# S5 output matrices built on VectorE behind the scan, and query decays broadcast through DRAM

## The chip, the cores and the metric

The kernel is one launch on one core of a Trainium2 chip. A core has five engines that each run their own stream of instructions in order: TensorE (PE in the profile, with its weight loads as PEld), VectorE (DVE), ScalarE (ACT), GpSimd (POOL) and SyncE (SP), which here only issues DMA transfers; POOL and ACT issue some too. Engines wait for one another through semaphores. The metric is the device time of one execution in microseconds, as a median over runs.

## What is computed

One step of a hybrid layer for 128 prompt tokens and 1024 sample tokens, model width 1024, in float32. Cut to what matters here:

```python
h    = norm(x) * (1 + sc1) + sh1
proj = h @ w_in                                   # 1024 x 2560
q, k, v, g, u = split(proj)                       # 4 x retention of 512, S5 input of 512
o_ret = bidirectional_retention(q, k, v, log_sigmoid(ret_decay), state_ret)
#   scores * exp(lg * (i - j));  states read with exp(lg * (i + 1)), written with exp(lg * (chunk - 1 - j))
y, s5_re, s5_im = bidirectional_s5(u, a, log_dt, b, c, d, s0)
#   s[t] = exp(a dt) s[t-1] + b u[t] (64 complex states, 32 groups of 16 channels); y = Re(c s) + d u
y = gelu(y); y = y * sigmoid(y @ w_glu + b_glu)
x = ln1(alpha * x + g1 * (concat(o_ret * silu(g), y) @ w_out))
x = ln2(alpha * x + g2 * squared_relu_mlp(norm(x) * (1 + sc2) + sh2))
```

## The kernel before

Each engine runs its instructions in the order in which the program writes them. For the stretch that matters (about 130 to 455 us of the span) that order comes from `weave` at the program's line 1097: it takes several tracks, each a generator that yields how many microseconds the piece just written should last, and always goes on with the track whose clock is lowest. The yields are numbers written by hand; they set the order and nothing else.

The tracks are these.

- `units(4, 20)`: the input projection, one unit for every 128 columns of `w_in`. A unit is three groups (384 tokens each) of 24 matmuls, `pu` at L205 to L207: eight blocks of the model width, three passes each, since weights and activations are split into a high and a low part. The split of the weights of unit i+1 is one copy `wh` on ACT (L197) and one subtraction `wl` on DVE (L198); the load `wr` of unit i+2 is issued on SP (L311). The first four units, which carry the S5 input u, are done before.
- `chain(s5_scan(), spill(), s5_w2_rest(), tables())`: the S5 scan on DVE. Seven steps over rows of SB, four operations of 128x1152 each (L667 to L670), 16 short steps on 128x64 (L684 to L687), and seven more of four row operations (L705 to L708). `spill` writes the scanned states to DRAM (SD, L890) and the final states to the output. `tables` makes the retention decays: the eight columns kd, and, as rows over 128 positions, RT (eight query decays) and DM (four decay matrices), in four batches of 128x384 through `emit_exp`, a chain of 16 DVE operations (L121 to L131).
- `mod_round(2, ...)`: eight pairs of matmuls `pm` (L266) with the modulation weights wa.
- `chain(s5_w2(), y_track(4))`: `build(u, d)` makes the output matrix W of channel block u and direction d (128x1152; twelve operations of 128x288, L978 to L980) on POOL for the first six of the eight and, through `s5_w2_rest`, on DVE after the scan for the last two. `finish(u, d)` multiplies it with Y on PE (`pK`, L992 and L993), writes W to DRAM (WD, L995) and after both directions the kernel matrix Kp (KD, L1011). Then `y_track`: `y_load(u)` issues on SP the loads of block u, eight of KD (L1056), the S5 input X from XD (L599), two of WD (L1062) and two of SD (L1063), into the buffers `late` and `ub`; `s5_y(u)` runs on PE 24 matmuls `py` (L1075 to L1077, eight groups of three, the third of each with the second W and states), on ACT the gelu, and POOL's queue writes YD and reads it back transposed (yT).

There is one set of these buffers. So the loads of block u+1 wait on SP until the matmuls of block u are done with them, and X of block u+1, which lies in the buffer that takes block u's gelu, until YD(u) has been written. After the weave PE goes on with the retention scores `psc` (L1129).

Of the kernel before, what the change touches and what calls it, by code (L numbers as in the profile page):

```python
# [9 lines left out]
F32 = mybir.dt.float32  # L10
# [7 lines left out]
P = 128  # L18
# [6 lines left out]
G = 32  # L25
# [6 lines left out]
def kernel(  # L32
# [52 lines left out]
    def t384(name, dt=F32):  # L85
        return sm.tile([P, 384], dt, tag="h", name=nm(name), bufs=4)

    def t512(name):
        return sm.tile([P, 512], F32, tag="rows", name=nm(name), bufs=1)

    def ct(name, shape, dt=F32):
        return const.tile(list(shape), dt, name=nm(name))

    def bc(ap, axis, n):
        ap = ap.unsqueeze(axis)
        shp = list(ap.shape)
        shp[axis] = n
        return ap.to_broadcast(shp)
# [11 lines left out]
    def chain(*tracks):  # L110
        for t in tracks:
            yield from t
# [542 lines left out]
    def s5_scan():  # L655
# [10 lines left out]
        for m in range(2, 9):  # L666
            tt(t1, bc(LRf, 3, NSB), row(m - 1), MUL)  # L667
            tt(row(m), row(m), t1, ADD)
            tt(t1, bc(LIf, 3, NSB), swp(row(m - 1)), MUL)
            tt(row(m), row(m), t1, ADD)  # L670
            yield 5.6

        R5 = SB.rearrange("p r d l (k s) -> p r d l k s", s=NSB)
        zr = st_[:, 0:64].rearrange("p (r d l) -> p r d l", r=2, d=2)
# [28 lines left out]
        for m in range(1, 8):  # L703
            prev = row(0) if m == 1 else cr
            tt(t1, bc(LIf, 3, NSB), swp(prev), MUL)  # L705
            tt(cr, bc(LRf, 3, NSB), prev, MUL)
            tt(cr, cr, t1, ADD)
            tt(row(m), row(m), cr, ADD)  # L708
            yield 5.6
        rel(st_, SE_)  # L710


# [190 lines left out]
        yield 0.0  # L903


    kd, kx = ct("kd", [P, 16]), ct("kx", [P, 48])
    RTf, DMf = ct("RT", [P, 1024]), ct("DM", [P, 512])
    RT = RTf.rearrange("p (a i) -> p a i", a=8)
    DM = DMf.rearrange("p (h i) -> p h i", h=4)
# [1 line left out]
    def tables():  # L911
# [15 lines left out]
        stt(lgb, p_, -2.0, m_, MUL, ADD)  # L927
        yield 3.0

        ts(kx[:, 0:4], lgb[:, 0:4], posP[:, 1:2], None, MUL)  # L930
        ts(kx[:, 4:8], lgb[:, 4:8], posP[:, 0:1], None, MUL)
        ts(kx[:, 8:16], lgb, 128.0, None, MUL)
        emit_exp(kd, kx[:, 0:16], kx[:, 16:32], kx[:, 32:48])
        yield 3.0

        pr = t512("pr")
        px, rx = pr[:, 0:256], pr[:, 256:512]
        ts(px[:, 0:128], posI, 1.0, None, ADD)
        ts(px[:, 128:256], posI, -1.0, 128.0, MUL, ADD)
        ts(rx[:, 0:128], posI, posP[:, 0:1], None, SUB)  # L940
        ts(rx[:, 128:256], rx[:, 0:128], -1.0, 0.0, MUL, ALU.max)
        ts(rx[:, 0:128], rx[:, 0:128], 0.0, None, ALU.max)
        x, t, k = (t384("tx") for _ in range(3))
        rows = [(RTf, a) for a in range(8)] + [(DMf, h) for h in range(4)]
        for i in range(4):
            part = rows[3 * i:3 * i + 3]
            for j, (f, a) in enumerate(part):
                xv = x[:, j * P:(j + 1) * P]
                if f is RTf:
                    ts(xv, px[:, 0:128] if a < 4 else px[:, 128:256], lgb[:, a:a + 1], None, MUL)  # L950
                else:
                    ts(xv, rx[:, 0:128], lgb[:, a:a + 1], None, MUL)
                    stt(xv, rx[:, 128:256], lgb[:, 4 + a:5 + a], xv, MUL, ADD)
            emit_exp(x, x, t, k)
            for j, (f, a) in enumerate(part):
                V.tensor_copy(f[:, a * P:(a + 1) * P], x[:, j * P:(j + 1) * P])
            yield 6.0
        tt(DM, DM, bc(ident, 1, 4), ADD)


# [2 lines left out]

    Ws, pks = {}, {}

    def build(u, d, e=PO.tensor_tensor):
        T = Ws[u, d] = slot("W2")
        Tv = T.rearrange("p (g k c) -> p g k c", g=8, k=9)
        for g in range(0, 8, 2):
            gs = slice(d * G + u * 8 + g, d * G + u * 8 + g + 2)  # L970
            gx = slice(u * 8 + g, u * 8 + g + 2)
            a_r, a_i = Ar[:, :, gs], Ai[:, :, gs]
            if d == 1:
                a_r, a_i = a_r[:, ::-1], a_i[:, ::-1]
            a_r, a_i = (bc(z.rearrange("p k g -> p g k"), 3, 16) for z in (a_r, a_i))
            Zv = t384("Z2")[:, 0:288].rearrange("p (g k c) -> p g k c", g=2, k=9)
            Tg = Tv[:, g:g + 2]
            e(Tg, a_r, bc(X1[:, gx], 2, 9), MUL)  # L978
            e(Zv, a_i, bc(X2[:, gx], 2, 9), MUL)
            e(Tg, Tg, Zv, ADD)  # L980

    def finish(u, d):
        extra[0] += 0.65
# [27 lines left out]
            ld(KD[u].rearrange("(s q) c x -> q c s x", q=4)[q], Kp[32 * q:32 * q + 16])  # L1011

    seq2 = [(u, d) for u in range(4) for d in range(2)]
    NPW, done = 6, []

    def s5_w2():

        for i, k in enumerate(seq2[0:NPW]):
            build(*k)
            yield 13.5  # L1020
            if i:
                finish(*seq2[i - 1])
        finish(*seq2[NPW - 1])
        while len(done) < 8 - NPW:
            yield 1.0
        for k in seq2[NPW:]:
            finish(*k)
        yield 3.0

    def s5_w2_rest():  # L1030
        for k in seq2[NPW:]:
            build(*k, tt)
            yield 6.5
            done.append(k)


    YD = drp.tile([4, 8, P, NCOL], F32, name="YD")
# [56 lines left out]
            yield YL2  # L1094

    YL1, YL2, NY = 22.0, 2.0, 4
    weave(units(4, 20), chain(s5_scan(), spill(), s5_w2_rest(), tables()), mod_round(2, 12.0, 60.0), chain(s5_w2(), y_track(NY)))
    rel(*hTh, *hTl)
    if stop <= 3:
        return  # L1100
# [611 lines left out]
```

## Time and profile before

| | us |
|---|---|
| runs (median of three) | 1500.23 (1498.35 to 1500.4) |
| the profiled execution: its own time | 1500.58 |
| the profiled execution: span | 1498.8 |
| PE busy over the span | 1385.7 (92%) |
| DVE busy | 839.1 (56%) |
| POOL busy | 317.2 (21%) |
| mean granted clock of PE | 0.963 |

PE is busy for nine tenths of the whole span, but that is an average over stages. The change lies in the stage from 130 to about 480 us, so the rows below are read from there. In the timeline of PE a row's duration overlaps with the next row's; the distance between starts is what a matmul costs. A count x2 or x8 in a row stands for that many hardware instructions merged into one.

### The profile page before, as it was taken

To read this page: it belongs to the slowest core of one execution; us is meant where nothing else is said; L and a number is where in the kernel's file an instruction comes from. 1 tells how busy PE (TensorE), PEld (TensorE's weight loads), DVE (VectorE), ACT (ScalarE), POOL (GpSimd) and SP (SyncE) were. 2 spreads that over 40 slices of the span, in tenths; PEclk is the share of its full clock that TensorE was granted. 3 is DMA by queue.
4 is the path that set the end of the run, shared out by engine and by line. 5 is a ranking of instruction groups with operands and counts; after the bars stand their busy time and mean duration, and the time that the engine had idled before them with its cause. 6 is when DMAs were issued, how large, how long until landed. Compare 5 with 4: busy or idle time off the path is not lost.

```text
span 1498.8 us, 19700 instructions
## 1 busy us (share of the span) xinstructions
PE 1385.7 (92%) x7630; PEld 1239.3 (83%) x7630; DVE 839.1 (56%) x1468; ACT 585.2 (39%) x973; POOL 317.2 (21%) x297
## 2 busy tenths in 40 slices
PE   5778997698988989999999999999999999999996
PEld 2468886598988778887999999989999998899995
DVE  6774699959304677677344443664443356543345
ACT  3434411012213563225344544444445444444451
POOL 0734586600214531253000010010001001000002
PEclk9789898799999999999999999999999999999998
DMA  9413344276786415138534434347443334734321
GB/s 327 99 58 97 116 151 134 80 181 197 185 198 241 153 47 181 67 119 266 197 126 156 120 105 143 109 138 228 141 127 113 119 106 141 253 113 141 113 84 43
DMA packets 194767, 214.10 MB, mean 143 GB/s; under 512 B 19761, under 2 KB 158705, under 8 KB 194161
## 3 DMA queue, kind: packets, MB, share of 16 engines
q1 hardware_dynamic: 186400, 197.99, 42.3%
q0 software_dynamic: 3328, 10.01, 2.2%
q10 hardware_dynamic: 4944, 4.83, 0.9%
q8 instruction: 60, 0.98, 0.3%
q14 instruction: 35, 0.28, 0.1%
HBM read 185.79 MB, written 27.02 MB: 142 GB/s over the span
## 4 chain that ended last, share of the span: by engine, by line
PE 50%; DVE 8%; issue 2%; ACT 2%; DMA 2%; POOL 1%; POOLq 0%; ACTq 0%; DVEq 0%; SPq 0%
PE ff L207 8%; PE ff L205 8%; PE ff L206 8%; PE acc L1542 8%; PE acc L1541 8%; PE acc L1540 8%; DMA w1r<-in_w_ff_dram 1%; DVE xr L1407 1%; DVE op L1406 1%; DVE st L154 1%; DVE st L155 1%; DVE hid L198 1%; ACT xr L1412 1%; DVE o L1585 0%; DMA RD<-xr 0%
## 5 line engine op out<-in xcount | busy, mean ns | idle before, releaser
L198 DVE TENSOR_TENSOR hid<-r,hid 128x384 fp32r<-128x384 f32 x96 | 67.5, 703 | 343.3 <-ACT hid L197 343.1
L205 PE MATMUL ff<-h,wh 128*128 128x384 f32 x768 | 258.9, 337 | 0.0
L207 PE MATMUL ff<-h,wl 128*128 128x384 f32 x768 | 257.8, 336 | 0.7 <-DVE wl L198 0.7
L206 PE MATMUL ff<-h,wh 128*128 128x384 f32 x768 | 257.3, 335 | 0.0
L1542 PE MATMUL acc<-wh,hid 128*128 128x512 f32 x564 | 223.0, 395 | 5.2 <-DVE hid L198 5.2
L1541 PE MATMUL acc<-wl,hid 128*128 128x512 f32 x564 | 222.3, 394 | 0.0
L1540 PE MATMUL acc<-wh,hid 128*128 128x512 f32 x564 | 220.8, 392 | 1.2 <-ACT hid L197 1.2
L205 PE MATMUL pu<-hTh,wh 128*128 128x384 f32 x480 | 169.8, 354 | 9.5 <-DVE hTh L195 7.7
L1518 ACT ACTIVATE r<-ff,bf 128x384 f32<-128x384 f32 x96 | 55.6, 579 | 308.7 <-PE ff L207 308.6
L207 PE MATMUL pu<-hTh,wl 128*128 128x384 f32 x480 | 166.4, 347 | 8.7 <-DVE wl L198 8.6
L206 PE MATMUL pu<-hTl,wh 128*128 128x384 f32 x480 | 167.2, 348 | 4.6 <-DVE hTl L198 4.5
L198 DVE TENSOR_TENSOR wl<-w1r,wh 128x1024 fp32r<-128x1024 f32 x96 | 117.5, 1224 | 59.7 <-ACT wh L197 55.1
L205 PEld LDWEIGHTS ff<-h,wh 128*128 128x128 f32 x768 | 144.2, 188 | 3.3 <-ACT wh L197 0.4
L206 PEld LDWEIGHTS ff<-h,wh 128*128 128x128 f32 x768 | 144.2, 188 | 2.9
L207 PEld LDWEIGHTS ff<-h,wl 128*128 128x128 f32 x768 | 144.1, 188 | 1.0 <-DVE wl L198 1.0
L1542 PEld LDWEIGHTS acc<-wh,hid 128*128 128x128 f32 x564 | 106.6, 189 | 29.4 <-DVE hid L198 7.0
L1540 PEld LDWEIGHTS acc<-wh,hid 128*128 128x128 f32 x564 | 106.7, 189 | 22.0 <-ACT hid L197 1.9
L1541 PEld LDWEIGHTS acc<-wl,hid 128*128 128x128 f32 x564 | 106.5, 189 | 20.7
L198 DVE TENSOR_TENSOR wl<-w2r,wh 128x1024 fp32r<-128x1024 f32 x95 | 120.1, 1265 | 1.0 <-PE acc L1542 0.6
L205 PEld LDWEIGHTS pu<-hTh,wh 128*128 128x128 f32 x480 | 94.4, 197 | 21.2 <-DVE hTh L195 9.5
L197 ACT ACTIVATE wh<-w1r 128x1024 fp32r<-128x1024 f32 x96 | 100.5, 1046 | 26.2 <-DMA w1r<-in_w_ff_dram 25.6
L207 PEld LDWEIGHTS pu<-hTh,wl 128*128 128x128 f32 x480 | 94.4, 197 | 9.9 <-DVE wl L198 9.9
(454 smaller groups left out, 2209.4 us busy)
## 6 DMA issues: line engine op xcount, KB each, us to landing
w1r<-in_w_ff_dram SPq DMA_DIRECT2D x96, 512.0 KB
w2r<-in_w_ff_dram SPq DMA_DIRECT2D x96, 512.0 KB
wa<-in_w_ada_dram SPq DMA_DIRECT2D x48, 512.0 KB
wr<-in_w_in_dram SPq DMA_DIRECT2D x20, 512.0 KB
WD<-W SPq DMA_DIRECT2D x8, 576.0 KB
SD<-SB SPq DMA_DIRECT2D x8, 576.0 KB
RD<-xr POOLq DMA_DIRECT2D x9, 512.0 KB, 3.1
x<-RD SPq DMA_DIRECT2D x9, 512.0 KB
```

What stands on the lines that cost most here:

```text
L154: V.bn_stats(st[:, 0], x[:, 0:512])
L155: V.bn_stats(st[:, 1], x[:, 512:1024])
L197: S.activation(hi, x, AF.Copy)
L198: (tt if leng == "v" else PO.tensor_tensor)(lo, x, hi.bitcast(F32), SUB)
L205: PE.matmul(out, lhsT=wh, rhs=xh, start=first, stop=False)
L206: PE.matmul(out, lhsT=wh, rhs=xl, start=False, stop=False)
L207: PE.matmul(out, lhsT=wl, rhs=xh, start=False, stop=last)
L1406: tt(po[hf], po[hf], gv[:, cs], MUL)
L1518: S.activation(r, pu[:, 0:384], AF.Relu, bias=bf1[:, f:f + 1])
L1540: PE.matmul(o, lhsT=hh[:, 0, tk], rhs=wh[:, cs], start=(f == 0), stop=False)
L1541: PE.matmul(o, lhsT=hh[:, 0, tk], rhs=wl[:, cs], start=False, stop=False)
L1542: PE.matmul(o, lhsT=hh[:, 1, tk], rhs=wh[:, cs], start=False, stop=(f == NF - 1))
```

## The change

All eight builds go to DVE, behind the scan, in the chain of the scan: `s5_w2` there builds and counts, and a new track `s5_finish` holds the products, each one build behind. A build is now seven operations: one of 128x1152 (L977 in the changed kernel) and three pairs of 128x384 (L980, L981). In `tables`, the query decays become eight more columns of kd (128x24); PE transposes them (`pq`, L941), ACT copies the result, and two DMAs on POOL's queue write it to DRAM (RTd) and read it back to all partitions (RT). DM takes two `emit_exp` of 128x256. The scan's yield goes from 5.6 to 6.3, and `mod_round` gets one more load ahead.

```diff
--- before.py
+++ after.py
@@ -668,7 +668,7 @@
             tt(row(m), row(m), t1, ADD)
             tt(t1, bc(LIf, 3, NSB), swp(row(m - 1)), MUL)
             tt(row(m), row(m), t1, ADD)
-            yield 5.6
+            yield 6.3
 
         R5 = SB.rearrange("p r d l (k s) -> p r d l k s", s=NSB)
         zr = st_[:, 0:64].rearrange("p (r d l) -> p r d l", r=2, d=2)
@@ -706,7 +706,7 @@
             tt(cr, bc(LRf, 3, NSB), prev, MUL)
             tt(cr, cr, t1, ADD)
             tt(row(m), row(m), cr, ADD)
-            yield 5.6
+            yield 6.3
         rel(st_, SE_)
 
 
@@ -903,7 +903,8 @@
         yield 0.0
 
 
-    kd, kx = ct("kd", [P, 16]), ct("kx", [P, 48])
+    kd = ct("kd", [P, 24])
+    RTd = drp.tile([8, P], F32, name="RTd")
     RTf, DMf = ct("RT", [P, 1024]), ct("DM", [P, 512])
     RT = RTf.rearrange("p (a i) -> p a i", a=8)
     DM = DMf.rearrange("p (h i) -> p h i", h=4)
@@ -927,34 +928,36 @@
         stt(lgb, p_, -2.0, m_, MUL, ADD)
         yield 3.0
 
+        kx = small("kx", 24)
         ts(kx[:, 0:4], lgb[:, 0:4], posP[:, 1:2], None, MUL)
         ts(kx[:, 4:8], lgb[:, 4:8], posP[:, 0:1], None, MUL)
         ts(kx[:, 8:16], lgb, 128.0, None, MUL)
-        emit_exp(kd, kx[:, 0:16], kx[:, 16:32], kx[:, 32:48])
-        yield 3.0
-
-        pr = t512("pr")
-        px, rx = pr[:, 0:256], pr[:, 256:512]
-        ts(px[:, 0:128], posI, 1.0, None, ADD)
-        ts(px[:, 128:256], posI, -1.0, 128.0, MUL, ADD)
+        stt(kx[:, 16:20], lgb[:, 0:4], posP[:, 0:1], lgb[:, 0:4], MUL, ADD)
+        stt(kx[:, 20:24], lgb[:, 4:8], posP[:, 1:2], lgb[:, 4:8], MUL, ADD)
+        emit_exp(kd, kx, small("kt", 24), small("kk", 24))
+        yield 4.5
+
+        pq = ps("pq")
+        PE.transpose(pq[0:8, 0:128], kd[:, 16:24], ident)
+        qd = t512("qd")
+        S.copy(qd[0:8, 0:128], pq[0:8, 0:128])
+        gl(RTd, qd[0:8, 0:128])
+        gl(RT, RTd.partition_broadcast(P))
+
+        rx, x, t, k = (t384("tx") for _ in range(4))
+        x, t, k = x[:, 0:256], t[:, 0:256], k[:, 0:256]
         ts(rx[:, 0:128], posI, posP[:, 0:1], None, SUB)
         ts(rx[:, 128:256], rx[:, 0:128], -1.0, 0.0, MUL, ALU.max)
         ts(rx[:, 0:128], rx[:, 0:128], 0.0, None, ALU.max)
-        x, t, k = (t384("tx") for _ in range(3))
-        rows = [(RTf, a) for a in range(8)] + [(DMf, h) for h in range(4)]
-        for i in range(4):
-            part = rows[3 * i:3 * i + 3]
-            for j, (f, a) in enumerate(part):
+        yield 1.0
+        for h in range(0, 4, 2):
+            for j in range(2):
                 xv = x[:, j * P:(j + 1) * P]
-                if f is RTf:
-                    ts(xv, px[:, 0:128] if a < 4 else px[:, 128:256], lgb[:, a:a + 1], None, MUL)
-                else:
-                    ts(xv, rx[:, 0:128], lgb[:, a:a + 1], None, MUL)
-                    stt(xv, rx[:, 128:256], lgb[:, 4 + a:5 + a], xv, MUL, ADD)
-            emit_exp(x, x, t, k)
-            for j, (f, a) in enumerate(part):
-                V.tensor_copy(f[:, a * P:(a + 1) * P], x[:, j * P:(j + 1) * P])
-            yield 6.0
+                ts(xv, rx[:, 0:128], lgb[:, h + j:h + j + 1], None, MUL)
+                stt(xv, rx[:, 128:256], lgb[:, 4 + h + j:5 + h + j], xv, MUL, ADD)
+            dm = DMf[:, h * P:(h + 2) * P]
+            emit_exp(dm, x, t, k)
+            yield 9.0
         tt(DM, DM, bc(ident, 1, 4), ADD)
 
 
@@ -963,21 +966,19 @@
 
     Ws, pks = {}, {}
 
-    def build(u, d, e=PO.tensor_tensor):
+    def build(u, d):
         T = Ws[u, d] = slot("W2")
         Tv = T.rearrange("p (g k c) -> p g k c", g=8, k=9)
-        for g in range(0, 8, 2):
-            gs = slice(d * G + u * 8 + g, d * G + u * 8 + g + 2)
-            gx = slice(u * 8 + g, u * 8 + g + 2)
-            a_r, a_i = Ar[:, :, gs], Ai[:, :, gs]
-            if d == 1:
-                a_r, a_i = a_r[:, ::-1], a_i[:, ::-1]
-            a_r, a_i = (bc(z.rearrange("p k g -> p g k"), 3, 16) for z in (a_r, a_i))
-            Zv = t384("Z2")[:, 0:288].rearrange("p (g k c) -> p g k c", g=2, k=9)
-            Tg = Tv[:, g:g + 2]
-            e(Tg, a_r, bc(X1[:, gx], 2, 9), MUL)
-            e(Zv, a_i, bc(X2[:, gx], 2, 9), MUL)
-            e(Tg, Tg, Zv, ADD)
+        gs, gx = slice(d * G + u * 8, d * G + u * 8 + 8), slice(u * 8, u * 8 + 8)
+        a_r, a_i = Ar[:, :, gs], Ai[:, :, gs]
+        if d == 1:
+            a_r, a_i = a_r[:, ::-1], a_i[:, ::-1]
+        a_r, a_i = (bc(z.rearrange("p k g -> p g k"), 3, 16) for z in (a_r, a_i))
+        tt(Tv, a_r, bc(X1[:, gx], 2, 9), MUL)
+        for k in range(0, 9, 3):
+            Zv, Tk = t384("Z2").rearrange("p (g k c) -> p g k c", g=8, k=3), Tv[:, :, k:k + 3]
+            tt(Zv, a_i[:, :, k:k + 3], bc(X2[:, gx], 2, 3), MUL)
+            tt(Tk, Tk, Zv, ADD)
 
     def finish(u, d):
         extra[0] += 0.65
@@ -1011,27 +1012,21 @@
             ld(KD[u].rearrange("(s q) c x -> q c s x", q=4)[q], Kp[32 * q:32 * q + 16])
 
     seq2 = [(u, d) for u in range(4) for d in range(2)]
-    NPW, done = 6, []
+    done = []
 
     def s5_w2():
-
-        for i, k in enumerate(seq2[0:NPW]):
+        for k in seq2:
             build(*k)
-            yield 13.5
-            if i:
-                finish(*seq2[i - 1])
-        finish(*seq2[NPW - 1])
-        while len(done) < 8 - NPW:
-            yield 1.0
-        for k in seq2[NPW:]:
+            yield 5.6
+            done.append(k)
+
+    def s5_finish():
+
+        for i, k in enumerate(seq2):
+            while len(done) < min(i + 2, 8):
+                yield 1.0
             finish(*k)
-        yield 3.0
-
-    def s5_w2_rest():
-        for k in seq2[NPW:]:
-            build(*k, tt)
-            yield 6.5
-            done.append(k)
+            yield 0.5
 
 
     YD = drp.tile([4, 8, P, NCOL], F32, name="YD")
@@ -1094,7 +1089,7 @@
             yield YL2
 
     YL1, YL2, NY = 22.0, 2.0, 4
-    weave(units(4, 20), chain(s5_scan(), spill(), s5_w2_rest(), tables()), mod_round(2, 12.0, 60.0), chain(s5_w2(), y_track(NY)))
+    weave(units(4, 20), chain(s5_scan(), spill(), s5_w2(), tables()), mod_round(2, 12.0, 60.0, 2), chain(s5_finish(), y_track(NY)))
     rel(*hTh, *hTl)
     if stop <= 3:
         return
```

With other yields and tracks the weave gives every engine another order. On PE, at the second output block: the last matmuls of py(1) in the kernel before (`py_3372`), and what follows them, the first group `pu` of unit 17.

```order
L1075 MATMUL py_3372<-ub_404_2885,late_3193 128x144
L1076 MATMUL py_3372<-ub_404_2885,late_3203 128x144
L1077 MATMUL py_3372<-late_3207,late_3206 128x144
L205 MATMUL pu_3413<-hTh_301,wh_3263 128x384
L206 MATMUL pu_3413<-hTl_302,wh_3263 128x384
L207 MATMUL pu_3413<-hTh_301,wl_3264 128x384
L205 MATMUL pu_3413<-hTh_312,wh_3263 128x384
L206 MATMUL pu_3413<-hTl_313,wh_3263 128x384
```

In the changed kernel py(1) (`py_3546` is its last tile) is followed by py(2) (`py_3581`).

```order
L1070 MATMUL py_3546<-ub_363_2654,late_3401 128x144
L1071 MATMUL py_3546<-ub_363_2654,late_3411 128x144
L1072 MATMUL py_3546<-late_3415,late_3414 128x144
L1070 MATMUL py_3581<-ub_363_2654,late_3564 128x144
L1071 MATMUL py_3581<-ub_363_2654,late_3574 128x144
L1072 MATMUL py_3581<-late_3578,late_3577 128x144
L1070 MATMUL py_3581<-ub_363_2654,late_3564 128x144
L1071 MATMUL py_3581<-ub_363_2654,late_3574 128x144
```

The unit matmuls that stood between the blocks have moved ahead of py(0), all but four groups, which stand between py(0) and py(1). The same holds between py(2) and py(3), and behind py(3) come the scores.

On DVE, behind the scan's last operation (L708), in the kernel before: one weight split (L198) and the first operations of the last two builds.

```order
L708 TENSOR_TENSOR SB_895<-SB_895,SE_896 128x64x18
L198 TENSOR_TENSOR wl_2605<-wr_2506,wh_2604 128x1024
L978 TENSOR_TENSOR W_382_2661<-Ar_119,X_24_123 128x288
L979 TENSOR_TENSOR Z_383_2662<-Ai_120,X_25_124 128x288
L980 TENSOR_TENSOR W_382_2661<-W_382_2661,Z_383_2662 128x288
L978 TENSOR_TENSOR W_382_2661<-Ar_119,X_24_123 128x288
L979 TENSOR_TENSOR Z_384_2666<-Ai_120,X_25_124 128x288
```

In the changed kernel, the first of eight builds in its new form (the first W goes through `W_349`).

```order
L708 TENSOR_TENSOR SB_895<-SB_895,SE_896 128x64x18
L198 TENSOR_TENSOR wl_2493<-wr_2398,wh_2492 128x1024
L977 TENSOR_TENSOR W_349_2549<-Ar_119,X_24_123 128x1152
L980 TENSOR_TENSOR Z_350_2551<-Ai_120,X_25_124 128x384
L981 TENSOR_TENSOR W_349_2549<-W_349_2549,Z_350_2551 128x8x48
L980 TENSOR_TENSOR Z_351_2554<-Ai_120,X_25_124 128x384
L981 TENSOR_TENSOR W_349_2549<-W_349_2549,Z_351_2554 128x8x48
L980 TENSOR_TENSOR Z_352_2557<-Ai_120,X_25_124 128x384
L981 TENSOR_TENSOR W_349_2549<-W_349_2549,Z_352_2557 128x8x48
L977 TENSOR_TENSOR W_354_2586<-Ar_119,X_24_123 128x1152
```

All eight builds now stand here, two, three, two and one of them between the weight splits, with the tables behind them.

On SP, from the second `y_load` on, in the kernel before: loads of block 1 and the weight load `wr` of a unit behind them, then block 2.

```order
L1056 DMA late_3193<-KD 16x8x128 x8
L599 DMA ub_404_2885<-XD 128x1152
L1062 DMA late_3203<-WD 128x8x128
L1063 DMA ub_404_2885<-SD 128x2x576
L1062 DMA late_3206<-WD 128x8x128
L1063 DMA late_3207<-SD 128x2x576
L311 DMA wr_3267<-in_w_in_dram 128x8x128
L1056 DMA late_3390<-KD 16x8x128 x8
L599 DMA ub_404_2885<-XD 128x1152
```

In the changed kernel, the loads of block 1 and of block 2.

```order
L1051 DMA late_3401<-KD 16x8x128 x8
L599 DMA ub_363_2654<-XD 128x1152
L1057 DMA late_3411<-WD 128x8x128
L1058 DMA ub_363_2654<-SD 128x2x576
L1057 DMA late_3414<-WD 128x8x128
L1058 DMA late_3415<-SD 128x2x576
L1051 DMA late_3564<-KD 16x8x128 x8
L599 DMA ub_363_2654<-XD 128x1152
```

No weight load stands between the blocks' loads any more; the last of them stands between block 0 and block 1.

## Rows read from the trace of the kernel before

**Rows 1.** Windows: stretch, length, busy time per engine, granted PE clock, DMA share, GB/s

```profile
184.00:363.00 179.00, 152.36 (x917) 136.64 (x916) 154.92 (x244) 28.13 (x60) 83.58 (x76) 0.91 0.52 155
...
419.30:422.70 3.40, 3.33 (x14) 3.36 (x15) 0.68 (x1) 1.50 (x3) 0.00 (x0) 0.53 0.26 63
422.70:426.70 4.00, 4.00 (x33) 4.00 (x33) 0.55 (x1) 1.93 (x2) 0.00 (x0) 0.97 0.00 0
...
426.21:448.61 22.40, 21.76 (x128) 21.54 (x127) 0.00 (x0) 3.26 (x7) 5.09 (x9) 1.00 0.92 219
```

**Rows 2.** Waits of PE from 170 to 480 us: total, times, longest

```profile
PE pK L992 <- POOL W L980: 14.8, 4, 5.0
PE pu L207 <- DVE wl L198: 8.6, 2, 4.6
```

**Rows 3.** VectorE in time order: start, duration, line, operation, tiles, [idle before]

```profile
172.28 1.86 DVE L667 TENSOR_TENSOR sct<-LR,SB 128x1152 f32<-128x1152 f32 x1
...
184.29 1.36 DVE L670 TENSOR_TENSOR SB<-SB,sct 128x1152 f32<-128x1152 f32 x1
...
204.54 1.75 DVE L670 TENSOR_TENSOR SB<-SB,sct 128x1152 f32<-128x1152 f32 x1
...
257.88 0.28 DVE L685 TENSOR_TENSOR SE<-SE,sct 128x64 f32<-128x64 f32 x1
...
307.40 1.36 DVE L708 TENSOR_TENSOR SB<-SB,SE 128x1152 f32<-128x1152 f32 x1
...
315.85 1.22 DVE L198 TENSOR_TENSOR wl<-wr,wh 128x1024 fp32r<-128x1024 f32 x1 [7.09 <-ACT wh L197]
316.99 0.45 DVE L978 TENSOR_TENSOR W<-Ar,X 128x288 f32<-128x288 f32 x1
...
326.46 0.46 DVE L980 TENSOR_TENSOR W<-W,Z 128x288 f32<-128x288 f32 x1
...
336.46 0.16 DVE L913 TENSOR_SCALAR lgx<-lgb 128x8 f32<-128x8 f32 x1
...
346.34 0.18 DVE L131 SCALAR_TENSOR_TENSOR kd<-kx,kd 128x16 f32<-128x16 f32 x1
```

**Rows 4.** PE in time order at the output blocks py, and the first scores

```profile
363.27 0.41 PE L1075 MATMUL py<-ub,late 128*128 128x144 f32 x2
...
392.33 0.48 PE L1077 MATMUL py<-late,late 128*128 128x144 f32 x2 [1.73 <-DMA late<-SD]
...
419.37 0.68 PE L1077 MATMUL py<-late,late 128*128 128x144 f32 x2 [2.89 <-DMA late<-SD]
...
448.61 0.51 PE L1077 MATMUL py<-late,late 128*128 128x144 f32 x2 [0.64 <-DMA late<-SD]
...
454.11 1.17 PE L1129 MATMUL psc<-qkv,qkv 128*128 128x128 f32 x9
```

**Rows 5.** SyncE's DMA issues in time order: start, time to issue, tiles, count

```profile
308.79 16.08 SPq L890 DMA_DIRECT2D SD<-SB  x8
...
342.86 4.50 SPq L1056 DMA_DIRECT2D late<-KD  x8
...
368.85 4.08 SPq L1056 DMA_DIRECT2D late<-KD  x8
...
397.50 4.25 SPq L1056 DMA_DIRECT2D late<-KD  x8
...
426.21 4.85 SPq L1056 DMA_DIRECT2D late<-KD  x8
```

**Rows 6.** PE in time order between 185 and 200 us, where groups meet other operations

```profile
185.18 0.45 PE L205 MATMUL pu<-hTh,wh 128*128 128x384 f32 x1
...
193.73 1.06 PE L266 MATMUL pm<-wa,stat 128*32 128x512 f32 x8
...
194.73 0.45 PE L205 MATMUL pu<-hTh,wh 128*128 128x384 f32 x1
...
199.12 0.64 PE L992 MATMUL pK<-W,Y 128*32 128x128 f32 x16
```

## The prediction

> **What bounds the kernel now.** I read the granted clock and busy shares by stretch first, then TensorE's (PE's) waits, then each engine's own rows in time order. All that the change touches lies between 170 and 480 us of the span. Up to 363 us PE is busy 152 of 179 us, at a mean granted clock of 0.91 [rows 1]; in the same stretch it waits 14.8 us, in four pieces, for the output matrices W that GpSimd (POOL) builds, and 8.6 us for weights that VectorE (DVE) splits [rows 2]. DVE is busy 155 of those 179 us: it runs the scan, and a row operation of the scan that takes 1.36 us alone takes 1.75 us where POOL builds beside it [rows 3]. So ahead of 363 us the matrices and the scan set PE's pace.
>
> From 363 us on something else does. The four output blocks py(0) to py(3) follow one another through a single set of buffers: block u+1's loads on SyncE (SP) start when block u's matmuls have let the buffers go, and the third matmul of block u+1 waits for the last of them. Let go to third matmul: 368.85 to 392.33, 397.50 to 419.37, 426.21 to 448.61, so 23.5, 21.9 and 22.4 us [rows 4, 5], with the 16 DMA engines 0.92 busy at 219 GB/s in the last of the three [rows 1]. The reader should see that PE's waits there are small (1.73, 2.89 and 0.64 us before the third matmuls) only because four to five groups of unit matmuls stand between two blocks. From the first matmul of py(0), 363.27, to the retention scores at 454.11 the length is one release (5.58), three refills (67.8), two blocks from third matmul to release (5.17 and 6.84) and a last one (5.50): 90.9 us. This chain is full already.
>
> **The change, part by part.** *Where the blocks stand.* In PE's order before, 30 groups of 24 unit matmuls lie between 185.18 us and py(0), and 14 more lie between the blocks. After, 40 groups lie ahead of py(0), four between py(0) and py(1), and none between py(1), py(2), py(3) and the scores. A group that follows another operation costs 4.39 us (194.73 to 199.12), one that follows a group 8.55 - 4.39 = 4.16 [rows 6]. Ahead of py(0) stand: 40 x 4.16 = 166.4; 18 places where the operation changes, 18 x 0.23 = 4.1; seven more pairs of modulation matmuls at 1.00, 7.0 (193.73 to 194.73); eight products pK at 0.64 as an upper bound, 5.1; four blocks of transposes, which I price like a pK, 2.6 (the bounds are nothing and that, since a few transposes are no larger than eight products). Sum 185.2; py(0) can start at 370.4 at the earliest, 7 us after 363.27, however quick the matrices are. Everything PE saves by not waiting for POOL is used to run ten more groups ahead of the block.
>
> *What DVE gains and takes on.* Without POOL's builds beside it the scan has 56 row operations at 1.39 (77.8 us) and 64 short ones at 0.31 (19.8), and some ten weight splits of 1.22 fall into it (12): from 172.3 it ends near 283, with a wait or two near 285, against 308.8 now [rows 3]. Here the rows show a partial slowing: 1.75 against 1.36, for one of POOL's instructions beside one of DVE's. [...]
>
> Two builds on DVE take 316.99 to 326.92 now, 4.97 each [rows 3]. The new form has one operation of 128x1152 (bounded by 1.36, the scan's of that size, from above and nothing gained from below) and six of 128x384 (a 128x288 one takes 0.45, so between 0.45 and 0.62): 4.1 to 5.1, I take 4.8. The builds of unit 0 are then ready near 295 while PE reaches the first pK near 307. The spill of the scan's states, 16.1 us of issue on SP [rows 5], stands ahead of the weight load for unit 15, so from 285 that load starts near 301 and its split comes at 313 to 314. The six remaining builds and two splits follow that on DVE: 314 + 6 x 4.8 + 2 x 1.2 = 345, against PE at the last pK at about 343 to 345. I put 1.5 us of waiting in, between nothing and 6.5 us (builds at 5.1, the split 3 us later, a late kd below). py(0) at 372, between 370.4 and 377.
>
> *The query decays.* Twelve rows of exponentials become eight columns in the small chain that takes 336.46 to 346.52 now [rows 3], a transpose on PE and two DMAs on POOL's queue. The chain now runs from 345 to 355 or 357; the transpose stands three groups ahead of py(0), near 358, so it costs nothing to 1 us, and a late one would hold PE by as much as it is late. The row tables RT are used well behind py(3), some 100 us after their DMAs are issued; a whole refill of 4 MB takes 22 us, so the two DMAs are hidden. The first block's loads, now issued near 350, had at most 20.4 us in the run before (342.86 to 363.27) and land by about 370: just hidden too, and within the 6.5 us above if not.
>
> *The chain after py(0).* PE runs four groups after py(0) and is out of work at 372 + 5.9 + 16.9 = 394.8. Unit 1 is let go at 372 + 5.6 = 377.6. I take 21.9 us per refill, the least of the three rows, since the weight loads that followed two of the refills now stand ahead of them. [...] Third matmul of py(1) 399.5, let go 406.3; of py(2) 428.2, let go 435.1; of py(3) 457.0; scores at 464.1. That is 10.0 us later than 454.11. What follows, the last unit's output through DRAM, the modulation weights' loads and POOL's gating, hangs on py(3) as before, so nothing is given back there.
>
> The profiled execution took 1500.58 us, span 1498.8, against a median of 1500.23; 1500.6 + 10.0 = 1510.6, and I say 1510.5. The bounds of the pieces: 370.4, full clock throughout and 21.9 give 370.4 + 5.6 + 65.7 + 10.3 + 5.5 = 457.5, or 1504.0; 377, and 23.5 per refill, give 377 + 5.6 + 70.5 + 13.7 + 7.2 = 474.0, or 1520.5.
>
> **The rivals.**
> [...]
>
> *Refills become quick (the other side, faster).* With no weight loads and no unit matmuls beside it a refill may take less. Its own loads are 3.25 MB, the output it waits for and the transposed copies another 1.15 MB. If only its loads counted, at 219 GB/s it would take 14.8 us: py(1)'s third matmul is then held by the unit groups to 395.5, and the chain is 395.5 + 6.8 + 14.8 + 6.8 + 14.8 + 7.2 = 445.9, 8.2 us early: 1492.4. It decides from 18.6 us per refill downward. Against it: the three refills differ by 1.6 us only, the third had no weight load for a unit behind it, and the DMA engines were 0.92 busy [rows 1, 5].
>
> *It comes out even.* py(0) at 370, the clock full, refills near 21.5: 1503 or just under. Each piece must fall at its lower end.
>
> *DVE is no quicker.* If the scan's 1.75 us had another cause than POOL, 56 x 0.36 = 20 us come back, the last pK waits near 360 and py(0) starts some 15 us later: 1526. Against: the operation at 184.29 has no build of POOL beside it and that at 204.54 has one [rows 3].
>
> **How the numbers follow.** Forecast 0.63; quick refills 0.12; even 0.09; half clock 0.12; DVE no quicker 0.04. About 0.2% (3 us) is what a measurement here can tell from no change, so faster 0.12, same 0.09, slower 0.79. The range 1500 to 1522 takes in the forecast's bounds, the even case and most of the half clock; what is left out is the quick refills, DVE no quicker and the tail of the half clock, 0.20.
>
> **What would show it.** Right: no wait of PE for POOL's W, waits for DVE's W under 7 us in all; the scan's last operation near 285; py(0) near 372; waits before the third matmuls of py(2) and py(3) of 18 to 22 us each on the loads of the states, about 5 before py(1); a granted clock near 0.5 at each restart; scores near 464. Wrong: refills under 19 us, a start of py(0) before 369, a wait of PE for W over 7 us, or time regained between 464 and the FFN.

## The result and the profile of the changed kernel

The changed kernel takes 1514.20 us (median of four, 1513.95 to 1514.92) against 1500.32 beside it: 1.0096 times as long, interval 1.0083 to 1.0108, 13.9 us slower. The forecast was 1510.5 with a range of 1500 to 1522. The profiled execution took 1514.92, span 1513.1.

The windows by stage (length, busy time of PE, PEld, DVE, ACT, POOL, granted clock of PE, DMA share, GB/s):

```profile
186.00:374.00 188.00, 185.10 (x1164) 172.71 (x1163) 149.81 (x267) 36.61 (x79) 11.07 (x18) 0.99 0.50 152
374.00:469.50 95.50, 50.73 (x291) 48.69 (x290) 7.52 (x21) 13.74 (x19) 15.36 (x27) 0.73 0.69 180
...
440.33:462.47 22.14, 2.10 (x8) 1.24 (x6) 0.00 (x0) 0.73 (x2) 5.10 (x9) 0.61 0.92 220
```

Up to the first output block PE is now busy for 185 of 188 us at a clock of 0.99, where it was busy for 152 of 179 at 0.91 [rows 1]: what the change was meant to do, it does. All of it and more is lost again in the next stage, where PE is busy for 51 of 95 us. Its waits from 170 to 500 us (total, times, longest):

```profile
PE py L1070 <- DMA ub<-XD: 20.3, 2, 10.5
PE py L1071 <- DMA ub<-SD: 17.3, 3, 7.9
PE py L1072 <- DMA late<-SD: 7.1, 3, 2.7
PE po L1192 <- POOL ub L1148: 3.1, 1, 3.1
PE pK L993 <- DVE W L981: 2.9, 2, 2.3
```

The 14.8 us of waiting for W and the 8.6 us for weight splits [rows 2] have become 2.9 and nothing. In their place stand 44.7 us of waiting for the loads of the output blocks; before, the third matmuls waited 5.3 us in all [rows 4]. Where it happens, in PE's time order (start, duration, line, operation, tiles, count, [idle before]):

```profile
187.13 0.45 PE L205 MATMUL pu<-hTh,wh 128*128 128x384 f32 x1
...
374.08 0.41 PE L1070 MATMUL py<-ub,late 128*128 128x144 f32 x2
...
402.15 0.82 PE L1072 MATMUL py<-late,late 128*128 128x144 f32 x2 [2.70 <-DMA late<-SD]
...
420.26 0.82 PE L1070 MATMUL py<-ub,late 128*128 128x144 f32 x2 [9.83 <-DMA ub<-XD]
428.95 0.82 PE L1071 MATMUL py<-ub,late 128*128 128x144 f32 x2 [7.87 <-DMA ub<-SD]
432.16 0.82 PE L1072 MATMUL py<-late,late 128*128 128x144 f32 x2 [2.39 <-DMA late<-SD]
...
462.47 0.85 PE L1072 MATMUL py<-late,late 128*128 128x144 f32 x2 [2.04 <-DMA late<-SD]
...
469.48 1.72 PE L1124 MATMUL psc<-qkv,qkv 128*128 128x128 f32 x14
```

And SP, where each block's loads start when the block before has let its buffers go:

```profile
288.57 16.13 SPq L890 DMA_DIRECT2D SD<-SB  x8
...
355.14 3.68 SPq L1051 DMA_DIRECT2D late<-KD  x8
...
379.67 4.31 SPq L1051 DMA_DIRECT2D late<-KD  x8
...
409.97 4.31 SPq L1051 DMA_DIRECT2D late<-KD  x8
...
440.33 4.30 SPq L1051 DMA_DIRECT2D late<-KD  x8
```

The two lists give the whole chain: 374.08, first release 5.59, then refill 22.48, block 7.82, refill 22.19, block 8.17, refill 22.14, last block 7.01, scores at 469.48. Before, the same chain ran from 363.27 to 454.11 [rows 4, 5]. So the scores come 15.4 us later, 10.8 of it from the later start and 4.6 inside the chain. The blocks that run at a low clock (granted 0.65, 0.62 and 0.78) add 5.5 there (5.17, 6.84 and 5.50 became 7.82, 8.17 and 7.01), and the three refills take 0.9 off (66.8 for 67.8). The products behind the scores start at 489.44 against 474.12, still 15.3 us late; 1.1 us comes back at the head of the MLP, which was not followed up.

VectorE behind the scan (start, duration, line, operation, tiles, count, [idle before]):

```profile
287.19 1.36 DVE L708 TENSOR_TENSOR SB<-SB,SE 128x1152 f32<-128x1152 f32 x1
...
294.34 1.35 DVE L977 TENSOR_TENSOR W<-Ar,X 128x1152 f32<-128x1152 f32 x1
...
298.80 1.35 DVE L977 TENSOR_TENSOR W<-Ar,X 128x1152 f32<-128x1152 f32 x1
...
315.02 1.23 DVE L198 TENSOR_TENSOR wl<-wr,wh 128x1024 fp32r<-128x1024 f32 x1 [11.69 <-ACT wh L197]
...
347.59 0.17 DVE L914 TENSOR_SCALAR lgx<-lgb 128x8 f32<-128x8 f32 x1
...
359.02 0.18 DVE L131 SCALAR_TENSOR_TENSOR kd<-kt,kd 128x24 f32<-128x24 f32 x1
```

The scan ends at 288.55 instead of 308.76, a build takes 298.80 - 294.34 = 4.46 us, the last is through at 347.6, and between them DVE stands idle for 11.69 us, since the weights it has to split are loaded behind the scan's spill.

### The profile page after: what moved, and what is told of

The parts are those of the page before. It is cut to its first block, busy times and chain, and to the rows that moved or that the text cites. A ratio compares the mean times of both kernels' runs of the same rounds, so it can differ in the third digit from the quotient of the medians.

```text
span 1513.1 us, 19613 instructions
## 1 busy us (share of the span) xinstructions
PE 1382.1 (91%) x7631; PEld 1239.5 (82%) x7631; DVE 812.1 (54%) x1450; ACT 585.5 (39%) x974; POOL 230.6 (15%) x227
## 4 chain that ended last, share of the span: by engine, by line
PE 52%; DVE 6%; ACT 2%; issue 2%; DMA 1%; POOL 1%; POOLq 0%; SPq 0%; DVEq 0%; ACTq 0%
PE ff L207 8%; PE ff L205 8%; PE ff L206 8%; PE acc L1537 8%; PE acc L1536 8%; PE acc L1535 7%; PE op L1389 1%; PE op L1388 1%; PE op L1390 1%; DMA w1r<-in_w_ff_dram 1%; DVE o L1580 1%; DVE hid L198 1%; DVE wl L198 0%; ACT o L1582 0%; DVE st L154 0%
## 5 line engine op out<-in xcount | busy, mean ns | idle before, releaser
L198 DVE TENSOR_TENSOR hid<-r,hid 128x384 fp32r<-128x384 f32 x96 | 67.5, 703 | 344.9 <-ACT hid L197 344.7
L198 DVE TENSOR_TENSOR wl<-w1r,wh 128x1024 fp32r<-128x1024 f32 x96 | 117.5, 1224 | 60.3 <-ACT wh L197 55.6
L198 DVE TENSOR_TENSOR wl<-w2r,wh 128x1024 fp32r<-128x1024 f32 x95 | 118.0, 1242 | 0.9 <-PE acc L1537 0.6
L197 ACT ACTIVATE wh<-w2r 128x1024 fp32r<-128x1024 f32 x96 | 100.3, 1045 | 0.0
```

The lines of the kernel that those rows point to most:

```text
L197: S.activation(hi, x, AF.Copy)
L198: (tt if leng == "v" else PO.tensor_tensor)(lo, x, hi.bitcast(F32), SUB)
```

## Experiments

The theory: the four blocks are a chain through one set of buffers; where the first stands in PE's order sets its start, the refills its pitch, and idle time before a block adds a cold start (in the kernel before 1.67 us after a wait of 2.89, at a granted clock of 0.53 for 3.4 us [rows 1, 4]). The rivals: the builds or the scan set the end (then the place of the blocks does not matter), or PE's sum of work does. "Scores" below is the first matmul of the retention scores, 469.48 in the changed kernel.

**The place of py(0) alone, in the kernel before.** One yield in `y_track`; who builds what stays.

```diff
-            yield YL1
+            yield 31.0 if u == 0 else YL1
```

> The kernel before with one planner number changed, builds and tables as they were: py(0) stands two groups (8.4 us) later in TensorE's order, and only two groups are left between py(2) and py(3). Theory (place of the blocks, not who builds): the chain starts 8.4 us later and its last block starts cold, so +8 to +11, 1508 to 1511. Rival (the builds and the scan set the end, the blocks have slack): within 2 us of the kernel before, 1500.

1511.05 us, 1.0068 (1.0048 to 1.0088), 10.2 us slower. On PE:

```profile
373.23 0.41 PE L1075 MATMUL py<-ub,late 128*128 128x144 f32 x2
...
453.07 0.82 PE L1076 MATMUL py<-ub,late 128*128 128x144 f32 x2 [6.95 <-DMA ub<-SD]
456.48 0.85 PE L1077 MATMUL py<-late,late 128*128 128x144 f32 x2 [2.60 <-DMA late<-SD]
464.58 0.61 PE L1129 MATMUL psc<-qkv,qkv 128*128 128x128 f32 x4
```

py(0) starts 10.0 us later than in [rows 4] and the scores come 10.5 us later. Two groups are 8.4 us of that; PE stood 1.6 us later already at the stage's first group (186.83 against 185.18), which no edit touches. The last block, cold after 11.4 us of waiting, takes 8.10 us and not 5.50: its pairs of matmuls stand 0.48 us apart up to 461.4 us and 0.245 behind that. Without touching builds or tables this gives most of the change's loss in the median too: the blocks have no slack here, and the rival of the builds falls.

**The other way round, in the changed kernel.** py(0) two groups earlier.

```diff
-            yield YL1
+            yield 14.0 if u == 0 else YL1
```

> The changed kernel with one planner number changed: py(0) stands two groups of unit matmuls (8.4 us) earlier in TensorE's order, and those two groups follow it. Theory (the start of the chain sets the end): py(0) could start at 365.5 and waits until its loads, issued from 355.1 to 364.4, have landed near 368 to 370; everything behind it comes 4 to 8 us earlier, 1506 to 1510. Rival (TensorE's work, not the chain, sets the end): no change, 1514. Second rival (the first loads land only at 374): no change, and a wait of 8 us before py(0).

1509.30 us, 1.0054 (1.0039 to 1.0069), as expected: faster than the changed kernel by 4.9 us by the medians and 6.3 by the ratios, each to the kernel before beside it.

```profile
369.30 0.72 PE L1072 MATMUL py<-late,late 128*128 128x144 f32 x2 [2.82 <-DMA late<-SD]
...
461.96 1.28 PE L1124 MATMUL psc<-qkv,qkv 128*128 128x128 f32 x10
```

The first loads land at 369.3; the changed kernel leaves them lying until its unit groups are through. The scores come 7.5 us earlier, of which 5.7 reach the end of the profiled execution (span 1507.4 against 1513.1).

**The clock.** Extra matmuls ahead of py(1) to py(3), 26, 112 and 112.

```diff
+        nf = (0, 26, 112, 112)[u]
+        if nf:
+            pfl = ps("pfl")
+            for i in range(nf):
+                PE.matmul(pfl[:, 0:384], lhsT=hTh[0][:, 0:128], rhs=hTh[0][:, 0:384], start=True, stop=True)
```

> The changed kernel with 26, 112 and 112 extra matmuls of 128x384 on TensorE ahead of py(1), py(2) and py(3) (their result is used nowhere), about 4.5 and 19.4 us each at 0.1735, which fit into the idle time there. Theory (chain of the blocks, with a part for the clock): the blocks start at the higher clock, third matmul to release falls from 7.8 and 8.2 to about 5.2 us, the last block from 7.0 to 5.5; start of py(0) and the refills of 22 us stay. The scores come 6 to 7 us earlier, 1507.5. Rival (the refill itself, not the clock, holds all of it): within 1 us of the changed kernel, 1514. Second rival (the extra work delays the blocks): 1516 or more.

1511.11 us, 1.0068 (1.0051 to 1.0085): less gain than the 1507.5 expected, and the interval touches that of the changed kernel, so that the gain at the end is not quite clear of noise. The blocks are. The windows of the three blocks from third matmul to release:

```profile
401.75:406.92 5.17, 5.17 (x42) 5.17 (x43) 0.00 (x0) 1.87 (x2) 0.00 (x0) 1.00 0.00 0
429.15:434.32 5.17, 5.17 (x42) 5.17 (x43) 0.00 (x0) 1.87 (x2) 0.00 (x0) 1.00 0.00 0
456.27:461.77 5.50, 5.50 (x45) 5.50 (x46) 0.00 (x0) 1.92 (x2) 0.00 (x0) 1.00 0.99 333
```

and of the same three in the changed kernel, py(1) after 4.6 us of waiting in two pieces, py(2) and py(3) after 20 us in three:

```profile
402.15:409.97 7.82, 7.82 (x42) 7.82 (x43) 0.00 (x0) 1.86 (x2) 0.00 (x0) 0.65 0.00 0
432.16:440.33 8.17, 8.17 (x42) 8.17 (x43) 0.00 (x0) 1.86 (x2) 0.00 (x0) 0.62 0.00 0
462.47:469.48 7.01, 7.01 (x44) 7.01 (x45) 0.00 (x0) 1.93 (x2) 0.00 (x0) 0.78 1.03 404
```

More work on PE makes the blocks shorter, by 2.65, 3.00 and 1.51 us, at refills that stay at 22 us; the scores come at 461.77, 7.7 us earlier. Only 3.8 us reach the end of the profiled execution (span 1509.3), less than the theory said. Behind the scores PE waits 5.3 us for the first query product on POOL, 3.1 in the changed kernel: POOL's queue holds the read of the last output ahead of them.

```profile
463.01 0.90 POOL L1081 DMA_DIRECT2D YD<-ub  x1 [17.97 <-DMA wa<-in_w_ada_dram]
472.90 4.17 POOL L1084 DMA_DIRECT2D late<-YD  x8 [8.98 <-PE pkb L1161]
480.73 0.79 POOL L1103 DMA_DIRECT2D bgl<-in_b_glu_dram  x1 [3.66 <-DMA late<-YD]
481.53 2.35 POOL L1153 TENSOR_TENSOR ub<-qkv,RT 128x1024 f32<-128x1024 f32 x1
```

From YD(3) to the first product it takes 18.5 us here, 16.3 in the changed kernel. That is 2.2 of the 3.9 us that are lost behind the scores; the rest was not followed up.

**The old tables with the builds on DVE.** The function `tables` of the kernel before, in the changed kernel.

```diff
-        PE.transpose(pq[0:8, 0:128], kd[:, 16:24], ident)
...
+        rows = [(RTf, a) for a in range(8)] + [(DMf, h) for h in range(4)]
...
```

> The changed kernel with the tables of the kernel before (query decays as rows on VectorE, no transpose, no DMA). Theory: the tables lie beside the chain, 1513 to 1515; the transpose of the decay columns held nothing. Rival (the transpose or its DMAs cost something on the path): 1 to 5 us faster.

Missed: 1533.18 us, 1.0218 (1.0201 to 1.0235), slower than the changed kernel by 19 us by the medians and 18 by the ratios. In time order on DVE, PE and ACT:

```profile
363.12 0.23 DVE L938 TENSOR_SCALAR pr<-posi 128x128 f32<-128x128 f32 x1 [6.92 <-ACT ub L841]
...
382.24 0.37 PE L297 MATMUL pg<-ident,gt 128*16 128x128 f32 x1 [10.89 <-DVE gt L293]
...
394.17 0.26 ACT L298 COPY gt<-pg 16x128 f32<-16x128 f32 x1 [22.29 <-DVE tx L953]
```

The tables' position rows (pr) share one buffer of 128x512 with the copies that the modulation makes. So DVE waits until PE has transposed the modulation's row copy, from 362.4 to 363.1 (the view names L841 of ACT, which ended at the same time and does not touch that buffer), PE's transpose pg ahead of py(0) waits for DVE, ACT's copy of the gates waits until the tables have let the buffer go, and the gelu of block 0 stands behind it. The test gives the position rows a buffer of their own:

```diff
-        pr = t512("pr")
+        pr = slot("pr")
```

> The kernel with builds on VectorE and the old tables, where the tables' position rows get a buffer of their own in place of the one buffer of 128x512 that they share with the modulation's row copies and its transposed gates. Theory (the 19 us of the old tables come from that one buffer: VectorE waits 6.9 us for it, TensorE's pg 10.9 us, ScalarE's copy of the gates 22.3 us, and the gelu of block 0 stands behind that copy): the tables start 7 us earlier, pg waits about 4 us, the gelu follows py(0) at once, 12 to 17 us come back, 1516 to 1522. Rival (the length of the tables on VectorE itself costs the 19 us): 1528 to 1533.

1521.50 us, 1.0148 (1.0118 to 1.0178).

```profile
378.77 0.37 PE L297 MATMUL pg<-ident,gt 128*16 128x128 f32 x1 [3.86 <-DVE gt L293]
...
379.24 0.26 ACT L298 COPY gt<-pg 16x128 f32<-16x128 f32 x1 [3.79 <-PE pg L297]
```

By the ratios 10 to 11 of the 18 us are that buffer. For the other 8 there is no run, only the trace: pg still waits 3.86 us for DVE, where the long tables stand ahead of the modulation's step; py(0) starts at 379.34, 5.3 us later than in the changed kernel; its block takes 7.98 us instead of 5.59, with pairs of matmuls 0.48 us apart up to 383.8 and 0.245 behind that; and the scores come 6.1 us later. So beside eight builds on DVE the new tables are worth their place. What they would be worth in the kernel before was not run.

**DVE's idle time.** The weight load of unit 15 ahead of the spill.

```diff
     def spill():
+        u_load(max(uraw) + 1)
```

> The changed kernel with one edit: the weight load of unit 15 is issued ahead of the spill. VectorE's idle time of 11.7 us before the split goes, and TensorE's order stays. Theory (TensorE's order sets the start of py(0), the builds only 2.9 us of it): the waits for W go, py(0) starts 2 to 3 us earlier, 1510 to 1512.5. Rival (the builds on VectorE are what delays the chain): 6 to 11 us faster.

1514.38 us, 1.0092 (1.0073 to 1.0111): no different from the changed kernel, and above what was expected, with one of its four runs (1512.47 to 1515.90) inside. In the trace, on DVE and PE, and PE's wait for W:

```profile
305.23 1.23 DVE L198 TENSOR_TENSOR wl<-wr,wh 128x1024 fp32r<-128x1024 f32 x1 [2.82 <-ACT wh L197]
...
372.44 0.41 PE L1071 MATMUL py<-ub,late 128*128 128x144 f32 x2
...
PE pK L994 <- DVE W L982: 2.3, 1, 2.3
```

The idle time falls from 11.69 to 2.82 us and the first loads go out 5.6 us earlier, at 349.52. But the waits for W, which were expected to go, do not: 2.3 of 2.9 us remain, now at the last product. py(0) starts 1.6 us earlier, and 0.9 of that is there already at the transpose of the final states, ahead of the builds (294.76 against 295.69). DVE had time to spare; PE's order holds the block.

**A second set of buffers.** Three free slots for the kernel matrix and both W of py(1) and py(3), loaded while the block before runs; only states and X are loaded between blocks.

```diff
-        W3 = ltile()
+        tl = [ltile() if u % 2 == 0 else slot("yW") for _ in range(3)]
...
+            if u == 0:
+                y_loadW(0)
+            y_loadX(u)
+            if u + 1 < n:
+                y_loadW(u + 1)
             yield YL1
             s5_y(u)
...
```

> The changed kernel with a second set of three buffers for the kernel matrix and the two W of a block (1.5 of the 3.25 MB that a block loads); only the states and X are still loaded between two blocks, states first. The order on TensorE stays. Theory (chain of blocks through one set of buffers): let go to third matmul falls from 22 to 11 to 14 us, py(1) is held by the unit groups in front of it to 396.5, the scores come near 437 to 446 instead of 469.5, 24 to 32 us earlier; some of it may be lost behind the scores, where GpSimd's queue waits for the last block's output (3 to 4 us were lost so when the blocks came 7.7 us earlier). 1482 to 1494. Rival (the 16 DMA engines' rate sets the refills, whatever the order of loads): the refills take 18 us or more, 1502 or more.

1492.30 us, 0.9945 (0.9928 to 0.9963), as expected: 22 us faster than the changed kernel, and faster than the kernel before. On PE, and on SP the first loads after a block has let its buffers go:

```profile
414.94 0.82 PE L1080 MATMUL py<-ub,late 128*128 128x144 f32 x2 [12.39 <-DMA yW<-KD]
...
436.25 0.82 PE L1080 MATMUL py<-ub,yW 128*128 128x144 f32 x2 [12.37 <-DMA ub<-XD]
...
444.62 1.61 PE L1140 MATMUL psc<-qkv,qkv 128*128 128x128 f32 x13
...
402.34 2.12 SPq L1065 DMA_DIRECT2D ub<-SD  x1
...
423.66 0.52 SPq L1065 DMA_DIRECT2D ub<-SD  x1
```

From let go to the first matmul of py(2) and of py(3) it is 12.6 us each, where the refill took 22, and the rival had 18 or more. (The first wait is put down to a load of yW, the matrix of py(3); py(2) does not read it, and the load of X that it does read went out just ahead, at 409.97.) The idle time before these blocks is 12.4 us instead of 20, py(1) waits no more, and the scores come 24.9 us earlier. Nothing but the loads and their order differs here: the order on PE, the builds and the tables are those of the changed kernel, so the refill is what the lost time hung on.

**Spread blocks on top.** py(0) two groups earlier, two groups between blocks, and the transposed read of an output one block later.

```diff
-            yield YL1
+            yield (14.0, 12.0, 12.0, 12.0)[u]
+            if u:
+                y_read(u - 1)
             s5_y(u)
...
```

> As the kernel with the second set of buffers, and the blocks spread again: py(0) two groups earlier, two groups of unit matmuls between py(0) and py(1), two and two behind them; the transposed read of a block's output is issued one block later. Theory (chain of blocks): another 4 to 6 us earlier than with the second set alone, 1477 to 1489, since the chain starts 5 us earlier and no block starts after more than 8 us of idle time. Rival (behind py(1) the sum of TensorE's work sets the end): the same time as the second set alone.

1489.58 us, 0.9919 (0.9896 to 0.9942): 2.7 us more by the medians, less than expected, with intervals that overlap, so that a gain is not shown. The windows from one block to the next, and a wait of SP's queue from 300 to 480 us:

```profile
392.20:415.30 23.10, 17.29 (x97) 17.03 (x97) 0.00 (x0) 3.71 (x6) 5.09 (x9) 0.80 0.89 194
415.30:435.80 20.50, 16.02 (x96) 15.70 (x96) 0.00 (x0) 3.66 (x5) 4.85 (x9) 0.92 1.01 219
...
SPq L599 <- DMA YD<-ub: 22.6, 3, 8.0
```

PE still waits 4 to 6 us before each block, so its sum of work does not decide, and py(0) starts only 3.1 us earlier. Two things can set the pitch of some 21 us a block. The DMA engines are 0.89 to 1.01 busy. And the blocks still form a chain: X of a block lies in the buffer that takes the gelu of the block before, so its load waits 7.5 us each time until YD is written. From py(2) to py(3) that is 7.48 us of matmuls, 8.6 until the load of X goes out and 4.5 until PE starts, 20.6 in all. No run here parts the two.

**And an earlier start.** The weight load ahead of the spill, a shorter yield for the builds (5.1), py(0) three groups earlier than in the changed kernel, and the second set's loads issued a little later, when a slot is free.

```diff
     def spill():
+        u_load(max(uraw) + 1)
...
-            yield 5.6
+            yield 5.1
...
             y_loadX(u)
+            yield 6.0
             if u + 1 < n:
                 y_loadW(u + 1)
-            yield (14.0, 12.0, 12.0, 12.0)[u]
+            yield (9.0, 7.0, 7.0, 8.0)[u]
```

> As the spread kernel with the second set, and besides the weight load of unit 15 is issued ahead of the spill of the scan's states, so that VectorE's builds need not wait for its split (11.7 us of idle time in the changed kernel), and the products pK stand up to one group earlier. Theory (start of the chain): the first loads start 4 to 7 us earlier and all behind them, 1472 to 1484. Rival (the spill or the first loads then land later, or the products wait for W): no gain over the spread kernel.

1482.11 us, 0.9882 (0.9864 to 0.9900), within the expected range: the first loads go out at 348.76, 6.4 us earlier than in the kernel above, and py(0) starts at 365.75, 4.9 us earlier. Which of its edits gives how much was not taken apart; the early weight load by itself gave nothing in the changed kernel.

**And POOL's queue behind the scores.** The last transposed read after the query products.

```diff
-            if u == n - 1:
-                y_read(u)
...
     ret_tok(1)
+    y_read(3)
```

> The kernel with the second set of buffers, spread blocks and the early weight load, and one edit more: the transposed read of the last block's output stands behind the query products with the decay rows on GpSimd's queue, no longer ahead of them. Theory (behind the scores TensorE waits 3.7 and 1.6 us for those products, which wait on the queue for the read): both waits go, 3 to 6 us faster than without the edit, 1476 to 1479. Rival (the read is then late for the gate's product): no gain, 1482.

1474.47 us, 0.9836 (0.9814 to 0.9858): 24 us faster than the kernel before, the fastest here, and some 7 us faster than without the edit, more than expected. The waits of 3.7 and 1.6 us for the products are gone. Another 1.9 us lay ahead of the scores in the profiled execution, which the edit does not touch. The scores stand at

```profile
435.97 1.28 PE L1145 MATMUL psc<-qkv,qkv 128*128 128x128 f32 x10
```

18 us ahead of the kernel before. What is left open: a second set of buffers with the builds still on POOL was not tried, since by my reading of the program the slots that it needs are taken there until later; how much of the 24 us needs the change is therefore not measured. Nor was the changed kernel run with one set of buffers and its blocks spread out as in the kernel before; with two groups moved behind py(0) it gained 5 to 6 us.

## Why the prediction was right

The sign and the mechanism were right: ten more groups of unit matmuls ahead of the first block, a chain behind it that has no slack. Step by step:

| step | forecast | measured |
|---|---|---|
| waits for W on PE | 1.5 (0 to 6.5) | 2.9 |
| one build on DVE | 4.8 | 4.46 |
| scan ends | near 285 | 288.55 |
| first loads issued | near 350 | 355.14 |
| py(0) | 372 | 374.08 |
| three refills | 65.7 | 66.8 |
| two blocks, third matmul to release | 13.7 | 16.0 |
| last block | 7.2 | 7.0 |
| scores | 464.1 | 469.48 |
| end (profiled execution) | 1510.6 | 1514.92 |

The 5.4 us by which the scores were missed have three parts, less 0.2 that the last block was quicker.

*The start, 2.1 us.* PE stood 1.95 us later already at the first group, 187.13 against 185.18 [rows 6], ahead of all that the change moves. In eight of the kernels above whose order is the same up to there the transpose of the final states stood between 293.0 and 296.2, so this is scatter between executions and no step of the sum. From that group to py(0) it took 186.95 us, and the sum with its waits said 186.7. That it fits so well is luck in part: the waits for W were 2.9 us and not 1.5, and the work, priced with upper bounds at 185.2, was 184.05.

*The blocks after idle time, 2.3 us.* The term that was mis-sized. I took the one cold start that the trace showed, 1.67 us after a wait of 2.89 (6.84 against 5.17 [rows 4]), for all three; two of the new ones cost 2.65, after 4.6 us of waiting, and 3.00, after 20.1. The forecast's 7.2 for the last block is 5.50 + 1.67, an estimate that no run shows; it took 7.01. The granted clock over the first two blocks was 0.65 and 0.62: 0.50 for the first 5.3 and 5.8 us, and 1.00 from 407.60 and 438.50 us on. The extra matmuls, which brought it to 1.00 throughout, gave the difference back. Half the clock for the whole of a block, which the chances put at 0.12, would by estimate take twice the 5.17 at a granted 1.00, so 10.3 us; no run shows that, and the measured 7.82 and 8.17 lie between the 6.84 of the forecast and that, nearer to the forecast. Over their length the three blocks show 0.65, 0.62 and 0.78, and the filled kernel shows what that costs here, 7.2 us in three blocks.

*The refills, 1.1 us.* I took 21.9 us, the least of three rows, because no weight load runs beside them any more; they came out at 22.48, 22.19 and 22.14, the mean of before less 0.3. One weight load still stood in the first of the three. So the weight loads had cost next to nothing by these rows.

Against that, 1.1 us came back far behind the scores, where I had put nothing.

The last build was late by 2.6 us and the first loads by 5. The first cost 0.6 us, PE's wait at the last product; the other 2.3 us of waiting for W came at the third product, at 320.97, from the weight split that DVE could start only at 315.02. The late loads cost nothing: the kernel with py(0) moved up shows the data there at 369.3, ahead of PE. The waits before py(2) and py(3) were 20.1 and 20.0 us, as forecast, but half of each was for X (9.83 and 10.51) and not for the states. That the scan would lose its slowing without POOL beside it is confirmed by every row operation at 1.35 to 1.36 us, where beside POOL's builds it had been 1.75 and 1.86 [rows 3]. The rival of quick refills fell: 22 us with PE idle and no weight loads; they were short only where there was less to load, 12.6 us with the second set of buffers. The rival that DVE would be no quicker fell with the scan's end.

One step was right for an incomplete reason: I counted the new tables as hidden and worth nothing. They are hidden, but the old ones would not have been, by 18 to 19 us, of which 10 to 11 came through the shared buffer.

## What to carry to other kernels

A stage in which every engine runs written orders can be freed of nearly all its waits and give nothing, or lose as here, if the next stage is a chain through a single set of buffers: look for its start in the order, since the time saved is spent on running other work ahead of it. Count, before moving work, what stands between two loads of the same buffers; work moved out from there was not saved here but replaced by idle time and a low clock (0.73 over the stage of the blocks). Where a chain of loads has no slack, try a few free buffers for the part of the load that does not depend on the block before: here 1.6 of 3.3 MB were worth 22 us, more than any reordering that was run, and 9 us less idle time of an engine upstream were worth nothing before that.

## What the hardware showed that I had not expected

A wait of 4.6 us cost a block nearly as much as one of 20.1: both blocks started at a granted clock of 0.50 (for 5.3 and 5.8 us; 0.65 and 0.62 over the whole block), and took 7.82 and 8.17 us from the third matmul on, where 5.17 is the time at a granted 1.00 and 6.84 that after a wait of 2.89. Keeping PE busy with useless matmuls through the waits made them 2.65 and 3.00 us quicker. The last block, also after 20 us, lost only 1.51; why less is not shown.

The three refills move 202 to 220 GB/s with the DMA engines 0.81 to 0.92 busy, while the window of the last block, with the modulation weights' loads in it, shows 404 GB/s at 1.03. The loads of a block come in 3072 rows of 512 bytes, 512 of 2304 and 128 of 4608, those weights in rows of 4096. In the refill of py(2) a row of 512 bytes took 41 ns on its DMA engine, in the window of the last block one of 4096 bytes 164 ns: eight times the bytes in four times the time. The refills reach about half the rate of the window with the longer rows; no run here changed the row length alone, so that this is the cause is not shown.

One buffer of 128x512 that a few short copies share tied DVE, PE and ACT together (waits of 6.9, 10.9 and 22.3 us with the old tables), and no engine's order shows it by itself.
